# A streaming encoder step on one core: the norm ahead of a gated feed-forward layer, taken apart into a weight on its operand and a factor on its products

## The chip, the cores and the metric

The kernel runs on one core of a Trainium2 chip. The metric is the time of one execution on the device in microseconds (us), as the median of several runs. The engines are TensorE (PE; its weight loads are shown as PEld), VectorE (DVE), ScalarE (ACT), GpSimd (POOL) and SyncE (SP), which here only issues DMAs. Each engine works through its own instructions in order; semaphores order the engines among each other.

## What is computed

One layer over 1024 new frames and 32 frames of a running stream, 1056 tokens of 1024 features. The part that the change touches is the end of the layer:

```python
h = x + mixed @ w_out
z = rmsnorm(h, norm_ffn_g)
h = h + (jax.nn.silu(z @ w_gate) * (z @ w_up)) @ w_down

def rmsnorm(x, g):
    y = x * rsqrt(mean(x * x, axis=-1) + 1e-6)
    return y * g
```

`w_gate` and `w_up` are 1024 x 2816, `w_out` 1024 x 1024, `w_down` 2816 x 1024, all in float32. The norm multiplies each feature by its weight g and each token by one factor r = rsqrt(mean(h²) + 1e-6). The factor is the same for all features of a token.

## The kernel before

Activations lie feature by feature: 128 features on the partitions, tokens along the columns. A float32 product is made of three fp32r products: each operand is split into a high part (ScalarE's copy to fp32r) and a low part (the difference), and high·high, high·low and low·high are added in PSUM. `split`, `block` and `low_part` do that (lines 245, 248, 1417, 1418, 1676, 1684).

**Tokens in pairs.** From `attn_out` on, the 1056 tokens are cut into four chunks of `CW` = 264 columns, two for each half p = 0, 1. The buffers come from pools: `pa` (14) and `pb` (16) hold tiles of 4 x 264 columns (`Q`), `tp` holds eight of 2 x 264 (`D`), which pass the residual's columns xt, the squares sq, the factor's na and nr, and t, s, y of the products. PSUM has seven banks for products.

**Output projection** (`out_proj`, from line 1546). Sixteen tiles n, the eight output blocks j for p = 0, then for p = 1. For each of the two chunks c: 24 matmuls (line 1430), VectorE adds the residual xt to the bank and writes h (line 1602), SP stores h to memory (line 1604; the down projection reads it again), ScalarE squares it (line 1605). With c = 0 VectorE also makes the low part of the next tile's weights (line 1418) and adds up the squares (line 1563). The tile of xt for n + 1 is loaded at the start of tile n (line 1557). In tiles 1 to 7 the weights of the first two units of gate and up are prepared.

**The operand of gate and up** (`pair_operand`, lines 1633 to 1679) is a generator that is advanced a step at a time between other work. It multiplies ones by the squares on TensorE (line 1638), takes Ln and Exp on ScalarE for r (lines 1639 to 1642, with a Newton step on VectorE, lines 1643 to 1645), scales the sixteen blocks of h with g and r on VectorE (line 1659), and then forms seven operands z from sums and differences of the four quarters of h (`B_SUMS`, line 1667), each with its zh (ScalarE, line 1676) and zl (VectorE, line 1684). For p = 0 it runs from tile 8 of the output projection on, in the order `EARLY`; for p = 1 it runs between the products of unit 0 and of the first half of unit 1, in the order of `ORDER`. An ACT table set with Ln and Exp is loaded at the start of `out_proj` (line 1568).

**Gate and up** (`ffn_up`). A unit f is 128 columns of gate and the same of up. The 2 x 2 block product of weights [gate, up] and operand is made by seven products instead of eight (`seven_products`, line 1736: seven of 12 matmuls, 84 in all, into four banks a to d). Order: unit 0 with p = 0, units 1 to 21 each with p = 0 and p = 1, unit 0 with p = 1. After products 1, 5 and 2 ScalarE copies the bank to t (line 1740), since products 7, 3 and 4 go on in the same banks; POOL combines the copies (lines 1743, 1744); VectorE adds the banks (line 1726); ScalarE takes Silu (lines 1750, 1755) and VectorE multiplies it by up (lines 1752, 1756). SP stores y (line 1810). While one unit runs, the weights of the next are prepared: sums on VectorE (ws, line 1705), high parts on ScalarE, low parts on POOL.

```python
            if i == 3:
                nc.scalar.activation(y1, banks["b"], AF.Silu)
                add(t1, banks["b"], t1)
                nc.vector.tensor_mul(y1, t1, y1)
            if i == 4:
                add(t2, banks["c"], t2)
                nc.scalar.activation(y0, t2, AF.Silu)
                nc.vector.tensor_mul(y0, banks["c"], y0)
```

In this whole part, up to the end of `ffn_up`, the order on each of the five engines is the order of the program.

**Down projection** (`ffn_down`) loads the stored y (line 1846), splits it, and adds the products to h, in new pools that take over the buffers and banks of the old ones as these come free.

Of the kernel before, what the change touches and what calls it, by code (L numbers as in the profile page):

```python
# [10 lines left out]
AF = mybir.ActivationFunctionType  # L11
ALU = mybir.AluOpType
# [17 lines left out]
CW = 264  # L30
# [24 lines left out]
ORDER = (1, 5, 2, 6, 7, 3, 4)  # L55
EARLY = (1, 5, 7, 4, 3, 2, 6)

STEPS = {0: "s0", 1: "p0", 2: "s3", 3: "p3", 4: "s4", 5: "p4", 8: "s1", 9: "s2 p1", 10: "p2", 11: "p5", 13: "p6"}
STEPS_1 = {7: "s0", 8: "s3 p0", 9: "s4 p3", 10: "s1 p4", 11: "s2 p1", 12: "p2 p5", 13: "p6"}
FIRST = {1: "s0", 2: "s1 p0", 3: "s2 p1", 4: "s3 p2", 5: "s4 p3", 6: "p4", 7: "p5 p6"}  # L60
BANK = {1: "a", 5: "b", 2: "c", 6: "d", 7: "a", 3: "b", 4: "c"}
# [79 lines left out]
class Builder:  # L141
# [1404 lines left out]
    def out_proj(self, w):  # L1546


        nc = self.nc
        xts, accs = [], []  # L1550
        work = None
        self.z = [{}, {}]

        def xt_load(p, j):
            xts.append(self.D("xt"))
            o = 2 * CW * p
            nc.sync.dma_start(xts[-1].rearrange("p c n -> p (c n)"), self.xT[j, :, o:o + 2 * CW])

        def sum_squares():

            if len(accs) == 2:
                x = accs.pop()
                nc.vector.tensor_add(accs[0], accs[0], x)

        order = [(p, j) for p in range(2) for j in range(8)]
        xt_load(0, 0)

        nc.scalar.preload_act_table_set("natural_log_exp_and_others")
        def tile(dt, s):
            return self.Q(self.pa, dt, s).rearrange("p c n -> p (c n)")[:, 0:NP].rearrange("p (k n) -> p k n", n=P)  # L1570

        preps = []
        for f in range(2):
            r = [tile(F32, "raw") for _ in range(2)]
            for x, src in zip(r, self.units[f]):
                nc.sync.dma_start(x, src)
            preps.append(self.unit_weights(r, nc.vector, tile if f else [self.wx] * 7))
            r = x = None

        def store(steps):  # L1580

            out = preps[1](steps)
            for i in list(out):
                hi, lo = out.pop(i)
                for a, x in enumerate((hi, lo)):
                    nc.sync.dma_start(self.w1d[ORDER.index(i), :, 4 * a:4 * a + 4, :], f32(x))

        h = {}
        for n, (p, j) in enumerate(order):
            self.fetch(3)  # L1590
            if n + 1 < len(order):
                xt_load(*order[n + 1])
            wj, xt = w, xts.pop(0)
            w, low = self.block(True) if n + 1 < len(order) else (None, None)
            sq = self.D("sq")
            for c in range(2):
                if j % 4 == 0:
                    h[j // 4, c] = self.Q((self.pa, self.pb)[p], s="h")
                ps = self.psd()
                self.block_products(ps, wj, lambda k: (x[:, 2 * (k % 2) + c, :] for x in self.mx[p, k // 2]), CW)  # L1600
                x = h[j // 4, c][:, j % 4, :]
                nc.vector.tensor_add(x, ps[:, :CW], xt[:, c, :])
                o = CW * (2 * p + c)
                nc.sync.dma_start(self.hd[j, :, o:o + CW], x)
                nc.scalar.activation(sq[:, c, :], x, AF.Square)
                if c == 0:
                    if low:
                        low(nc.vector)
                    sum_squares()
                    if n in FIRST:  # L1610
                        preps[0](FIRST[n])
                    if n == 8:
                        work = self.pair_operand(0, h0, accs.pop(), EARLY)
                        h0 = None
                elif n in FIRST:
                    store(FIRST[n])
                for _ in range((c if n == 8 else 1 + c) if work else 0):
                    next(work, None)
            accs.append(sq)
            if j == 7:  # L1620
                for k in range(4):
                    del self.mx[p, k]
                if p == 0:
                    h0, h = h, {}
            if n == 14:
                self.turn = 0
                self.third = self.unit_load(2)
        sum_squares()
        for _ in work:
            pass  # L1630
        self.unit, self.work = preps[0](""), self.pair_operand(1, h, accs.pop(), ORDER)

    def pair_operand(self, p, h, acc, order):

        nc = self.nc
        a, r = self.D("na"), self.D("nr")
        for c, t in enumerate((self.pst(), self.psd())):
            nc.tensor.matmul(t[:, :CW], self.ones, acc[:, c, :], start=True, stop=True)
            nc.scalar.activation(r[:, c, :], t[:, :CW], AF.Ln, bias=self.eps_rms, scale=1.0 / 1024)
            nc.scalar.activation(a[:, c, :], t[:, :CW], AF.Identity, bias=self.eps_rms, scale=1.0 / 1024)  # L1640
        acc = None
        nc.scalar.activation(r, r, AF.Exp, scale=-0.5)
        nc.vector.scalar_tensor_tensor(a, a, -0.5, r, op0=ALU.mult, op1=ALU.mult)
        nc.vector.tensor_mul(a, a, r)
        nc.vector.scalar_tensor_tensor(r, a, 1.5, r, op0=ALU.add, op1=ALU.mult)
        a = None
        yield
        left = {q: sum(q in B_SUMS[i] for i in order) for q in h}
        normed = set()
        low = None  # L1650
        pool = (self.pa, self.pb)[p]
        for i in order:
            terms = B_SUMS[i]
            for q in terms[:2]:
                if q not in normed:
                    normed.add(q)
                    for k in range(4):
                        x = h[q][:, k, :]
                        nc.vector.scalar_tensor_tensor(x, x, self.g("norm_ffn_g", 4 * q[0] + k), r[:, q[1], :], op0=ALU.mult,  # L1659
                                                       op1=ALU.mult)  # L1660
                    yield
            if len(normed) == 4:
                r = None
            x = h[terms[0]]
            if len(terms) > 1:
                x = self.Q(self.pb, s="sum")
                nc.vector.tensor_tensor(x, h[terms[0]], h[terms[1]], terms[2])
            for q in terms[:2]:
                left[q] -= 1
                if left[q] == 0:  # L1670
                    del h[q]
            yield
            if low:
                self.low_part(p, pool, *low)
            hi = self.Q(pool, FR, "zh")
            nc.scalar.copy(hi, x)
            low = i, x, hi
            x = None
            yield
        self.low_part(p, pool, *low)  # L1680

    def low_part(self, p, pool, i, x, hi):
        lo = self.Q(pool, FR, "zl")
# [33 lines left out]
    def seven_products(self, w, p, between):  # L1717
# [4 lines left out]
        t, s, y = self.D("t"), self.D("t"), self.D("y")  # L1722
        t1, t2, t5 = t[:, 0, :], t[:, 1, :], s[:, 0, :]
        y0, y1 = y[:, 0, :], y[:, 1, :]
        copies = {1: t1, 5: t5, 2: t2}
        add = lambda out, a, b, op=ALU.add: nc.vector.tensor_tensor(out, a, b, op)  # L1726
        for i in ORDER:
# [19 lines left out]
            if i == 7:  # L1747
                add(t2, banks["a"], t2, ALU.subtract)
            if i == 3:
                nc.scalar.activation(y1, banks["b"], AF.Silu)  # L1750
                add(t1, banks["b"], t1)
                nc.vector.tensor_mul(y1, t1, y1)
            if i == 4:
                add(t2, banks["c"], t2)
                nc.scalar.activation(y0, t2, AF.Silu)
                nc.vector.tensor_mul(y0, banks["c"], y0)
        return y

    def unit_load(self, f):
# [17 lines left out]
    def ffn_up(self):  # L1777
# [7 lines left out]
        for n, f in enumerate(order):  # L1785
# [7 lines left out]
            for p in (0, 1) if 0 < n < NFF else (n > 0,):  # L1793

                def between():
                    nonlocal w, step
                    if prep and step in steps:
                        w = prep(steps[step])
                    step += 1
                    if n < 2 and p == 0 and n + step > 2:  # L1800
                        for _ in range(1 + (n + step > 3)):
                            next(work, None)

                if n == p == 1:
                    for _ in work:
                        pass
                y = self.seven_products(cur, p, between)
                o = 2 * CW * p
                queue = nc.scalar if n == NFF else nc.sync
                queue.dma_start(self.hidd[f, :, o:o + 2 * CW], y.rearrange("p c n -> p (c n)"))  # L1810
                y = None
            if n + 3 < len(order):
                raws.append(self.unit_load(order[n + 3]))
            cur = prep = None
        self.z = w = None

    def ffn_down(self, region):
        nc = self.nc
# [304 lines left out]
```

## Time and profile before

| | |
|---|---|
| median of 3 runs | 1569.53 us (1568.97 to 1569.88) |
| the profiled execution's own time | 1572.19 us |
| its span, first to last instruction | 1570.4 us |
| PE busy | 1513.8 us (96%) |
| DVE busy | 957.5 us (61%) |
| ACT busy | 593.2 us (38%) |
| POOL busy | 482.1 us (31%) |
| mean granted clock of TensorE | 0.985 of full speed |
| longest groups of the chain that ended last | matmuls of gate and up (line 1736) 26%, of output and down projection (line 1430) 18%, of the input projection (line 429) 11% |

A profile shows one execution; its time lies close to the median, and differences are formed against the execution itself. An engine's busy time says how much it has to do, not whether the end waits for it: for that, one looks for stretches in which TensorE, the busiest engine, stood idle, and for what released it.

### The profile page before, as it was taken

Reading aid. Unit: us, or ns where it says so; the run is one execution under the profiler, and the core shown is the slowest. Engines: PE = TensorE matmul, PEld = TensorE weight load, DVE = VectorE, ACT = ScalarE, POOL = GpSimd, SP = SyncE. Lnnn points to the kernel's source line nnn. Section 1 sums busy time; section 2 is a strip of 40 time slices with the busy share of each in tenths; the row PEclk is TensorE's granted clock in tenths of the full one; section 3 lists DMA queues with packets and bytes.
Section 4 is the critical chain, followed back from the end, with each engine's and each line's share of the span. In section 5 each row is a group of like instructions: output and inputs, shape, how many; then the busy total and the mean of one; then the engine's idle time right before and its main releaser. Section 6 shows DMA issues by size and latency. Waiting matters only on the chain.

```text
span 1570.4 us, 27321 instructions
## 1 busy us (share of the span) xinstructions
PE 1513.8 (96%) x10622; PEld 1477.1 (94%) x10622; DVE 957.5 (61%) x1743; ACT 593.2 (38%) x1219; POOL 482.1 (31%) x482
## 2 busy tenths in 40 slices
PE   8999999989999999988998999999999999999997
PEld 7999998979999998888997999999999999999996
DVE  7799998668776566355797544444444444234236
ACT  4411212375655444233543333333333342122115
POOL 2200000433432212310000655565555553122222
PEclk9999999999999999989999999999999999999999
DMA  8312232434633467856854222222222237223213
GB/s 251 120 41 81 87 100 75 132 76 134 203 105 112 119 208 223 266 185 184 262 151 159 82 80 70 71 75 82 82 82 82 82 102 232 83 79 112 84 63 111
DMA packets 212880, 193.54 MB, mean 123 GB/s; under 512 B 13018, under 2 KB 185846, under 8 KB 212751
## 3 DMA queue, kind: packets, MB, share of 16 engines
q1 hardware_dynamic: 212015, 189.91, 39.6%
q8 instruction: 83, 1.36, 0.4%
q0 software_dynamic: 576, 1.62, 0.3%
q14 instruction: 46, 0.38, 0.1%
q10 hardware_dynamic: 160, 0.27, 0.0%
HBM read 135.08 MB, written 56.68 MB: 122 GB/s over the span
## 4 chain that ended last, share of the span: by engine, by line
PE 65%; DVE 6%; ACT 3%; issue 3%; DMA 2%; POOL 1%; SPq 0%; DVEq 0%; ACTq 0%; POOLq 0%
PE pd L1736 26%; PE pd L1430 18%; PE pd L429 11%; PE po L1112 2%; PE ps L1073 2%; PE pt L1095 2%; PE pd L1899 1%; PE pt L251 1%; DVE gate L1495 1%; DMA xt<-xT 1%; DVE h L1659 1%; DVE ml L1499 1%; PE pd L1924 1%; DVE wlo L1418 1%; PE pt L1274 0%
## 5 line engine op out<-in xcount | busy, mean ns | idle before, releaser
L1736 PE MATMUL pd<-zh,whl 128*128 128x264 f32 x2464 | 455.6, 286 | 10.5 <-ACT t L1740 9.6
L1736 PEld LDWEIGHTS pd<-zh,whl 128*128 128x128 f32 x2464 | 386.3, 190 | 11.5 <-ACT t L1740 10.1
L1736 PE MATMUL pd<-zl,whl 128*128 128x264 f32 x1232 | 352.4, 286 | 0.0
L429 PE MATMUL pd<-xl,whi 128*128 128x352 f32 x832 | 270.6, 325 | 0.5 <-POOL xl L539 0.5
L429 PE MATMUL pd<-xh,whi 128*128 128x352 f32 x832 | 271.0, 326 | 0.0
L429 PE MATMUL pd<-xh,wlo 128*128 128x352 f32 x832 | 270.9, 326 | 0.0
L1736 PEld LDWEIGHTS pd<-zl,whl 128*128 128x128 f32 x1232 | 234.3, 190 | 0.0
L1726 DVE TENSOR_TENSOR t<-pd,t 128x264 f32<-128x264 f32 x176 | 75.4, 429 | 202.1 <-POOL t L1744 154.1
L248 POOL TENSOR_TENSOR whl<-ws,whl 128x512 fp32r<-128x512 f32 x105 | 135.6, 1292 | 147.9 <-ACT whl L245 147.9
L429 PEld LDWEIGHTS pd<-xl,whi 128*128 128x128 f32 x832 | 156.8, 188 | 2.0 <-POOL xl L539 0.8
L429 PEld LDWEIGHTS pd<-xh,whi 128*128 128x128 f32 x832 | 156.8, 188 | 1.4
L429 PEld LDWEIGHTS pd<-xh,wlo 128*128 128x128 f32 x832 | 156.8, 188 | 0.7
L766 DVE SCALAR_TENSOR_TENSOR acc<-cu,wdw,acc 128x1024 f32<-128x1024 f32 x120 | 147.3, 1284 | 0.2
L1875 DVE TENSOR_TENSOR h<-pd,h 128x352 f32<-128x352 f32 x96 | 49.7, 523 | 138.3 <-PE pd L1430 138.2
L1430 PE MATMUL pd<-hl,whi 128*128 128x352 f32 x360 | 116.1, 323 | 0.0
L1430 PE MATMUL pd<-hh,whi 128*128 128x352 f32 x360 | 116.1, 322 | 0.0
L1430 PE MATMUL pd<-hh,wlo 128*128 128x352 f32 x360 | 116.1, 322 | 0.0
L245 ACT CAST whl<-ws 128x512 fp32r<-128x512 f32 x115 | 71.4, 621 | 74.7 <-DVE ws L1705 72.1
L248 POOL TENSOR_TENSOR wlo<-raw,whi 128x1024 fp32r<-128x1024 f32 (+1 forms) x31 | 63.9, 2062 | 100.3 <-ACT whi L245 84.7
L245 ACT CAST whi<-raw 128x1024 fp32r<-128x1024 f32 (+1 forms) x47 | 45.0, 957 | 112.0 <-PE pd L429 79.2
L1418 POOL TENSOR_TENSOR wlo<-raw,whi 128x640 fp32r<-128x640 f32 x24 | 39.4, 1643 | 131.9 <-ACT whi L1417 117.0
L1743 POOL TENSOR_TENSOR t<-t,t 128x264 f32<-128x264 f32 x44 | 34.0, 773 | 146.3 <-ACT t L1740 146.3
(349 smaller groups left out, 3061.1 us busy)
## 6 DMA issues: line engine op xcount, KB each, us to landing
raw<-in_w_in SPq DMA_DIRECT2D x35, 512.0 KB, 4.0
hidd<-y SPq DMA_DIRECT2D x43, 264.0 KB, 2.0
hid<-hidd SPq DMA_DIRECT2D x18, 528.0 KB, 4.5
gd<-gate SPq DMA_DIRECT2D x48, 176.0 KB, 1.8
q<-qd SPq DMA_DIRECT2D x32, 256.0 KB, 5.0
raw<-in_w_down SPq DMA_DIRECT2D x24, 320.0 KB, 3.3
raw<-in_w_gate SPq DMA_DIRECT2D x13, 512.0 KB, 4.9
raw<-in_w_up SPq DMA_DIRECT2D x13, 512.0 KB, 4.7
```

Of the source, the lines that this page charges most:

```text
L245: nc.scalar.copy(hi, src)
L248: (lo_engine or nc.gpsimd).tensor_tensor(lo, src, f32(hi), ALU.subtract)
L429: nc.tensor.matmul(ps[:, :n], lhs, b, start=(m == 0), stop=(m == total - 1))
L766: nc.vector.scalar_tensor_tensor(acc[:, 0:NP], cu[:, j:j + NP], w(j), acc[:, 0:NP], op0=ALU.mult, op1=ALU.add)
L1073: nc.tensor.matmul(s[:, 512 * j:512 * j + e - o], q[:, m, qs], k[:, o:e], start=(m == 0), stop=(m == 1))
L1095: nc.tensor.transpose(t[:, o:o + P], lt[n, b][:, P * kb:P * kb + P], self.ident)
L1418: low = lambda engine: engine.tensor_tensor(lo, r, f32(hi), ALU.subtract)
L1430: self.nc.tensor.matmul(ps[:, :n], a[:, k, :], b, start=(m == 0), stop=(m == total - 1))
L1726: add = lambda out, a, b, op=ALU.add: nc.vector.tensor_tensor(out, a, b, op)
L1736: nc.tensor.matmul(banks[b], x[:, k, :], z[:, k, :], start=first and k == m == 0, stop=i not in copies and k == 3 and m == 2, skip_group_c ...
L1743: nc.gpsimd.tensor_tensor(t2, t2, t5, ALU.add)
L1875: nc.vector.tensor_add(s, ps[:, :CH], s)
```

## The change

The weight g and the factor r of the norm are taken apart. VectorE writes h into the buffer of xt, SP stores it from there, and ScalarE writes h·g as a copy with a scale for each partition. The operands z are formed from h·g without r, so `pair_operand` no longer waits for the factor and no longer scales. The factor r is made by a function of its own, `norm_factor`: for p = 0 in tile 8 as before, for p = 1 after the third product of unit 1 (before: of unit 0), and both stay in their `tp` buffers to the end of `ffn_up`. In `seven_products` gate is multiplied by r ahead of Silu, and the finished y by r once more, which is up's factor. Operand 2 of p = 1, the first of the new order `LATER`, is formed in tile 14 of the output projection. The steps of the generators are spread anew: one a chunk in the output projection, one a product in unit 0 and the first half of unit 1.

```diff
+LATER = (2, 1, 5, 6, 7, 3, 4)
...
-                x = h[j // 4, c][:, j % 4, :]
-                nc.vector.tensor_add(x, ps[:, :CW], xt[:, c, :])
+                x = xt[:, c, :]
+                nc.vector.tensor_add(x, ps[:, :CW], x)
                 o = CW * (2 * p + c)
                 nc.sync.dma_start(self.hd[j, :, o:o + CW], x)
+                nc.scalar.activation(h[j // 4, c][:, j % 4, :], x, AF.Copy, scale=self.g("norm_ffn_g", j))
                 nc.scalar.activation(sq[:, c, :], x, AF.Square)
...
                     if n == 8:
-                        work = self.pair_operand(0, h0, accs.pop(), EARLY)
+                        self.norm_factor(0, accs.pop())
+                        work = self.pair_operand(0, h0, EARLY)
                         h0 = None
...
-                for _ in range((c if n == 8 else 1 + c) if work else 0):
+                if work:
                     next(work, None)
+                    if n == 15:
+                        next(work, None)
+                if n == 13 and c:
+                    ahead = self.pair_operand(1, h, LATER, 1)
+                if n == 14:
+                    next(ahead)
...
-        self.unit, self.work = preps[0](""), self.pair_operand(1, h, accs.pop(), ORDER)
+        self.unit, self.work, self.squares = preps[0](""), ahead, accs.pop()
...
-                    for k in range(4):
-                        x = h[q][:, k, :]
-                        nc.vector.scalar_tensor_tensor(x, x, self.g("norm_ffn_g", 4 * q[0] + k), r[:, q[1], :], op0=ALU.mult,
-                                                       op1=ALU.mult)
-                    yield
...
             if i == 3:
-                nc.scalar.activation(y1, banks["b"], AF.Silu)
+                nc.vector.tensor_mul(y1, banks["b"], r[:, 1, :])
+                nc.scalar.activation(y1, y1, AF.Silu)
                 add(t1, banks["b"], t1)
                 nc.vector.tensor_mul(y1, t1, y1)
             if i == 4:
                 add(t2, banks["c"], t2)
-                nc.scalar.activation(y0, t2, AF.Silu)
+                nc.vector.tensor_mul(y0, t2, r[:, 0, :])
+                nc.scalar.activation(y0, y0, AF.Silu)
                 nc.vector.tensor_mul(y0, banks["c"], y0)
+                nc.vector.tensor_mul(y, y, r)
...
-                    if n < 2 and p == 0 and n + step > 2:
-                        for _ in range(1 + (n + step > 3)):
-                            next(work, None)
+                    if n < 2 and p == 0:
+                        next(work, None)
+                    if n == 1 and step == 3:
+                        self.norm_factor(1, self.squares)
+                        self.squares = None
```

## Rows read from the trace of the kernel before

**Rows 1.** Stretches: length, busy (x instructions) by engine, clock, DMA share, GB/s.

```profile
725.90:825.90 100.00, 97.51 (x771) 96.06 (x772) 78.49 (x123) 45.89 (x75) 0.00 (x0) 0.98 0.62 191
825.90:877.30 51.40, 40.87 (x285) 39.89 (x283) 38.42 (x55) 19.68 (x35) 12.31 (x12) 0.87 0.36 118
877.30:1293.00 415.70, 415.70 (x3418) 415.52 (x3418) 190.85 (x350) 157.65 (x353) 249.11 (x226) 1.00 0.28 81
```

**Rows 2.** Stretches of one product each, unit 1 and unit 2.

```profile
837.00:855.30 18.30, 13.21 (x85) 13.00 (x85) 15.49 (x27) 7.01 (x10) 1.58 (x2) 0.81 0.39 125
855.30:872.90 17.60, 13.05 (x88) 12.84 (x87) 14.71 (x18) 7.14 (x12) 5.50 (x5) 0.81 0.04 16
872.90:884.90 12.00, 11.11 (x88) 10.61 (x87) 6.79 (x10) 4.33 (x10) 9.36 (x9) 1.00 0.41 110
884.90:895.10 10.20, 10.20 (x86) 10.20 (x85) 6.00 (x12) 4.73 (x11) 5.96 (x7) 1.00 0.08 29
```

**Rows 3.** TensorE's waits, 825 to 880: total us, times, longest us.

```profile
PE pd L1736 <- ACT t L1740: 9.6, 2, 5.1
```

**Rows 4.** Stretches after two stops of TensorE.

```profile
848.00:854.00 6.00, 5.93 (x27) 5.93 (x28) 5.96 (x10) 1.65 (x4) 1.34 (x2) 0.50 0.80 220
1298.00:1301.50 3.50, 3.50 (x14) 3.50 (x13) 0.34 (x2) 0.62 (x1) 1.27 (x1) 0.52 0.91 251
```

**Rows 5.** Timeline of ScalarE: start us, duration us, instruction, idle before.

```profile
830.96 0.48 ACT L1639 ACTIVATE nr<-pt,eps_rms 128x264 f32<-128x264 f32 x1 [1.57 <-PE pt L1638]
832.43 0.66 ACT L1642 ACTIVATE nr<-nr 128x528 f32<-128x528 f32 x1
843.16 1.28 ACT L1750 ACT_TABLE_LOAD   x1
844.45 0.39 ACT L1750 ACTIVATE y<-pd 128x264 f32<-128x264 f32 x1
847.32 0.42 ACT L1755 ACTIVATE y<-t 128x264 f32<-128x264 f32 x1 [1.52 <-DVE t L1726]
847.65 0.64 ACT L1740 COPY t<-pd 128x264 f32<-128x264 f32 x2
```

**Rows 6.** Timeline of VectorE, units 0 and 1.

```profile
833.12 0.71 DVE L1643 SCALAR_TENSOR_TENSOR na<-na,nr 128x528 f32<-128x528 f32 x1 [4.96 <-ACT nr L1642]
836.22 3.32 DVE L1659 SCALAR_TENSOR_TENSOR h<-h,vec,nr 128x264 f32<-128x264 f32 x8
839.46 0.43 DVE L1726 TENSOR_TENSOR t<-pd,t 128x264 f32<-128x264 f32 x1
839.80 1.25 DVE L1667 TENSOR_TENSOR sum<-h,h 128x1056 f32<-128x1056 f32 x1
840.97 0.43 DVE L1726 TENSOR_TENSOR t<-pd,t 128x264 f32<-128x264 f32 x1
846.86 0.43 DVE L1726 TENSOR_TENSOR t<-pd,t 128x264 f32<-128x264 f32 x1
```

**Rows 7.** Timeline of ScalarE, the convolution's norm.

```profile
348.01 1.28 ACT L815 ACT_TABLE_LOAD   x1
350.32 1.28 ACT L820 ACT_TABLE_LOAD   x1
```

**Rows 8.** Timeline of VectorE, first weight sum for unit 2.

```profile
865.91 1.28 DVE L1705 TENSOR_TENSOR ws<-raw,raw 128x512 f32<-128x512 f32 x2
```

**Rows 9.** Timeline of ScalarE, a product of a later unit.

```profile
1008.79 0.38 ACT L1740 COPY t<-pd 128x264 f32<-128x264 f32 x1 [0.32 <-PE pd L1736]
```

**Rows 10.** Timeline into the down projection, SP's store and TensorE's wait.

```profile
1286.26 0.32 SPq L1810 DMA_DIRECT2D hidd<-y  x1
...
1297.69 0.43 PE L1430 MATMUL pd<-hh,whl 128*128 128x352 f32 x1 [1.93 <-DVE y L1756]
```

**Rows 11.** DMA issues, 735 to 826: count, KB each, median us to landing.

```profile
hd<-h SPq DMA_DIRECT2D x30, 132.0 KB, 3.0
xt<-xT SPq DMA_DIRECT2D x14, 264.0 KB, 4.4
```

More of the change, by code (lines that the diff above doesn't have):

```diff
@@ L1551, in out_proj @@
         work = None
-        self.z = [{}, {}]
+        self.z, self.r = [{}, {}], {}
         def xt_load(p, j):
@@ L1588, in out_proj @@
         h = {}
+        ahead = None
         for n, (p, j) in enumerate(order):
@@ L1630, in out_proj, with norm_factor @@
             pass
-        self.unit, self.work = preps[0](""), self.pair_operand(1, h, accs.pop(), ORDER)
-    def pair_operand(self, p, h, acc, order):
+        self.unit, self.work, self.squares = preps[0](""), ahead, accs.pop()
+    def norm_factor(self, p, acc):
         nc = self.nc
@@ L1640, in pair_operand @@
             nc.scalar.activation(a[:, c, :], t[:, :CW], AF.Identity, bias=self.eps_rms, scale=1.0 / 1024)
-        acc = None
         nc.scalar.activation(r, r, AF.Exp, scale=-0.5)
@@ L1645, in pair_operand @@
         nc.vector.scalar_tensor_tensor(r, a, 1.5, r, op0=ALU.add, op1=ALU.mult)
-        a = None
-        yield
-        left = {q: sum(q in B_SUMS[i] for i in order) for q in h}
-        normed = set()
+        self.r[p] = r
+    def pair_operand(self, p, h, order, early=0):
+        nc = self.nc
+        left = {q: sum(q in B_SUMS[i] for i in order) for q in ((0, 0), (0, 1), (1, 0), (1, 1))}
         low = None
         pool = (self.pa, self.pb)[p]
-        for i in order:
+        for n, i in enumerate(order):
             terms = B_SUMS[i]
-            for q in terms[:2]:
-                if q not in normed:
-                    normed.add(q)
-                    for k in range(4):
-                        x = h[q][:, k, :]
-                        nc.vector.scalar_tensor_tensor(x, x, self.g("norm_ffn_g", 4 * q[0] + k), r[:, q[1], :], op0=ALU.mult,
-                                                       op1=ALU.mult)
-                    yield
-            if len(normed) == 4:
-                r = None
             x = h[terms[0]]
@@ L1671, in pair_operand @@
                     del h[q]
-            yield
+            if len(terms) > 1:
+                yield
             if low:
@@ L1677, in pair_operand @@
             low = i, x, hi
-            x = None
+            x = hi = None
             yield
-        self.low_part(p, pool, *low)
+            if n < early:
+                self.low_part(p, pool, *low)
+                low = None
+                yield
+        if low:
+            self.low_part(p, pool, *low)
     def low_part(self, p, pool, i, x, hi):
@@ L1724, in seven_products @@
         y0, y1 = y[:, 0, :], y[:, 1, :]
+        r = self.r[p]
         copies = {1: t1, 5: t5, 2: t2}
@@ L1814, in ffn_up @@
             cur = prep = None
-        self.z = w = None
+        self.z = self.r = w = None
     def ffn_down(self, region):
```

## The prediction, made before the changed kernel was run

> **What bounds the kernel now.** I read the page first, then the chain of waits, then stretches and the timeline by engine. TensorE is the longest busy row by far, so time is won only where it stands idle or runs at half clock. By stage [rows 1], it is idle for 2.5 of the output projection's 100 us (725.9 to 825.9), most of it in that stage's start, which the change leaves alone; in units 2 to 21 of gate and up (877.3 to 1293) it is never idle; but in 825.9 to 877.3 it is busy for 40.9 of 51.4 us at a granted clock of 0.87. That stretch is where the second half's factor and operand are made. A product of 84 matmuls takes 10.20 us when nothing is late (the last of [rows 2]). Against that the first half of unit 1 lasted 18.3 (8.1 lost), its second half 17.6 (7.4 lost), the first half of unit 2 12.0 (1.8 lost): 17.3 us in all. In the first two, 9.6 us are two waits of TensorE, 5.1 and 4.5, for ScalarE's copy of a bank (t, L1740) [rows 3]. The other 5.9 are mostly the half clock behind each: 27 matmuls took 0.22 us apiece instead of 0.1215, at a granted 0.50, the 1.2 GHz level [rows 4].
>
> Why was the copy late? ScalarE works in order, and ahead of the copy (847.65) stood the second Silu (847.32), idle until VectorE's t (L1726) [rows 5]. VectorE had stood empty 4.96 us for the factor's Exp, then worked through three factor instructions, eight of sixteen scalings (L1659), a sum and two low parts before it came to that t at 846.86 [rows 6]. So VectorE, through ScalarE's queue, is what ends last there.
>
> **The change, part by part.** Starts below are chained from [rows 2, 5, 6], start to start where instructions overlap: on VectorE 1.17 for 1056 columns (839.80 to 840.97), 0.35 for 264, 0.405 for a scaling, 3.1 for the factor's three; on ScalarE 0.98 for 1056, 0.36 for Ln and its like, 0.53 for Exp, 1.28 for a table load; on TensorE 1.46 for twelve matmuls.
>
> *Unit 0.* VectorE loses its empty 4.96 us, the factor and the scalings; three sums, three low parts, four adds, the first y and two new multiplications by the factor remain, 9.9 us from 828.4, with 2.3 of waits for POOL and ScalarE. The second Silu then starts at 840.6 instead of 847.3, the copy at 840.9. TensorE, past the sums of squares (0.94, moved here), wants it at 842.9. The 5.1 us are gone, with 2.0 to spare.
>
> *Unit 1, first half.* VectorE still has the last y, the new y·r (0.62) and the sum for operand 3: ends 843.3. ScalarE's copy zh of it ends 844.3, and the copy for operand 5 behind it 844.7, wanted at 844.3: 0.4 lost. Now the second half's factor stands in ScalarE's queue, ahead of the copy for operand 2. Before, its Ln and Exp ran under a table set loaded in the output projection; now a Silu has run in between. In the convolution's norm, Ln (L815) after another function took a load, and Exp (L820) after that Ln a second [rows 7]. So: load 1.28, four instructions of 0.36, load 1.28, Exp 0.53, and the copy ends at 849.5, wanted at 846.2: 3.4 lost. The third load, for Silu, hides: VectorE is later.
> By the Trainium skill ("ScalarE: Activation LUTs", Table sets) one set holds both exp and ln, so Ln then Exp would need one load, and the sum below would be 1.3 us better. [Rows 7] show two in this kernel, which I take.
>
> *Unit 1, second half.* From 849.3 VectorE does the factor (3.1), two low parts (2.3) and ten short instructions with their waits; the second Silu starts at 857.8, the copy behind it at 858.1. TensorE, if its clock stays up, wants it at 856.8 (1.7 lost by its end, then 0.9 for the next copy); if the 3.4 us take the clock down, TensorE itself is later and loses about 2.6 in slow matmuls instead. After the 1.93 us before the down projection the clock was 0.52 [rows 4, 10]; I take it so. Either way 2.6.
>
> *Unit 2.* Its weights are prepared behind that: the first sum (ws) starts at 859.2, 4.6 us before unit 2 begins at 863.8; before it was 865.91 against 872.9, 7.0 ahead [rows 2, 8]. The 1.8 us lost there grow to about 4.
>
> Sum: 0.4 + 3.4 + 2.6 + 4 = 10.4 lost, against 17.3: **6.9 us won**. Ends: 14.3 (only 3 lost: Ln and Exp share a load, the clock holds, the weights are in time) and 1 (each late step half as long again).
>
> *Output projection.* VectorE loses 16 scalings (6.5 us) in its second half and gains one low part; ScalarE gains 32 copies. No row has that form; the nearest with a column as operand is Ln, 0.48 [rows 5], the nearest without is the copy of a bank, 0.32 start to start; I take 0.48, 15 us over 100 in which ScalarE is busy 46 [rows 1]. Behind a copy stand the square and the next block's high part, wanted some 3 us later by the low part: covered. If not, 0.4 us a tile, 6 us. VectorE's relief shortens TensorE's waits for a low part there by 0.3, my estimate from the 2.5 us of idle time. The residual's buffer now waits for its store; that is a rival below.
>
> *Units 2 to 21.* Three VectorE instructions a product, about 0.43 + 0.43 + 0.70, some 62 us over 416 in which VectorE is busy 191 and TensorE always [rows 1]. The tightest use is again the copy behind the second Silu: it stood idle 0.32 us for TensorE [rows 9], so a Silu 0.5 later moves it by 0.2, and TensorE wants it four blocks, 5.8 us, after its own part is done. Cost 0; if that cover of over 4 us were gone, 0.5 us on each of 39 products, 20 us. The factors keep two of eight buffers; a product uses three, so two products still fit. SP's store of y comes 1.1 us later and the raw loads behind it too; they are read a unit (20 us) later: 0.
>
> *Into the down projection.* Here nothing hides it. TensorE stood 1.93 us for the bank that VectorE's last y frees [rows 10], then ran at half clock. That bank is now free only after y0·r: 0.45 later. The ten loads of the hidden rows stand on SP behind the store of unit 21's y (1286.26) [rows 10], which waits for the new y·r: 0.7 later, and ScalarE's splits of them stand ahead of the last Silus. I take **1.2 lost**; ends 0.4 (the splits have slack) and 2.5 (both, and a changed order).
>
> Net: -6.9 - 0.3 + 1.2 = -6.0. The profiled execution took 1572.19, 0.17% over the median of 1569.53; the difference carries over: 1566.2 beside the profile, **1563.5** for the median.
>
> **The rivals.** *Only moved (0.18).* The factor's chain in unit 1 is longer than I chain it, since ScalarE now stands between two waits of TensorE: both loads cost as much again (2.6), or VectorE's fourteen short instructions stretch as the last two of the factor's three did (1.2 each where one alone takes 0.71, [rows 6]). Of the 6.9 between 1 and 3.9 are left: 1566.5 to 1569.5. Against: Silu started 1.29 us after its load did [rows 5].
> The Trainium skill (same page, What ACT_TABLE_LOAD costs) counts 2.66 us a switch with its drain, the rule for this rival; the row agrees with the load alone.
>
> *All gone (0.13).* Every late step fits: 1555 to 1558. For it: VectorE is then no longer what ScalarE waits for in unit 0. Against: the two loads.
>
> *Slower by the residual's buffer (0.08).* xt was free once VectorE had added; now it holds until the store has landed. If the next load got the buffer of the tile just left, SP would wait with all behind it: 0.9 for add and issue, 3.0 for the store, 4.4 for the load [rows 11], 8.3 us, of 9.9 until the low part behind the add is late (a tile and a half, 8.7, and 1.2 of slack). At medians that fits; from 1.6 us above them it decides, and at 2.2 above it costs 0.6 on each of 15 tiles, 9 us: 1573. Against: at most six of eight buffers live, so the oldest is two tiles back.
>
> **How the numbers follow.** The forecast, 0.61, spans 1559 to 1566.4. About 0.2% (3.1 us) is what a measurement here can tell from no change: faster is below 1566.4, slower above 1572.7. Faster 0.61 + 0.13 = 0.74, same 0.18, slower 0.08. The range leaves out the slower case and the tail of the best: 1557.5 to 1569.
>
> **What would show it.** In the profile after: no wait of TensorE for t near 843; a wait of 3 to 4 us two blocks on, behind two table loads; the next under 2 us; TensorE busy throughout 880 to 1285; VectorE's share up by some 3 points; a longer stop before the down projection. Wrong would be: TensorE waiting in units 3 to 21, SP waiting before xt, or one load around Ln and Exp.

## The result, and the profile after

The changed kernel takes **1583.52 us** (median of 6; 1581.19 to 1585.75) against 1569.25 for the kernel before beside it (6 runs): ratio 1.0090, 95% interval 1.0074 to 1.0105. It is 0.9% slower; the prediction was 1563.5 and at most 1569. The profiled execution took 1582.46 with a span of 1580.2 (before 1572.19 and 1570.4), so the two profiles differ by 9.8 us of span and the medians by 14.3: before was profiled in one of its slower executions, after in one of its faster, and the ledger below, which is of the spans, holds 4.5 us less than the medians do.

The page of the changed kernel, busy time by engine:

```profile
PE 1517.3 (96%) x10622; PEld 1477.4 (93%) x10622; DVE 1030.5 (65%) x1843; ACT 604.1 (38%) x1254; POOL 479.3 (30%) x482
```

TensorE does the same 10622 matmuls; no other engine is near full. TensorE's waits from the output projection into the down projection (waited for, total us, times, longest), after:

```profile
PE pd L1745 <- ACT t L1749: 12.6, 24, 4.0
PE pt L1648 <- DVE sq L1564: 3.0, 1, 3.0
PE pd L1431 <- DVE t L1735: 3.0, 1, 3.0
PE pd L1745 <- POOL whl L249: 1.9, 1, 1.9
```

The first answers to [rows 3], two waits that made 9.6; now they are 24, most of them of 0.2 us. The stretches that answer to [rows 1]: the output projection; the 51.4 us from the start of unit 0, which hold units 0 and 1 and part of unit 2; the rest of gate and up:

```profile
725.90:825.90 100.00, 95.18 (x746) 93.88 (x746) 72.29 (x104) 59.15 (x107) 0.00 (x0) 0.97 0.58 182
827.46:878.90 51.44, 44.61 (x329) 43.20 (x328) 36.50 (x50) 25.39 (x44) 17.37 (x15) 0.93 0.38 125
878.90:1302.35 423.45, 415.74 (x3374) 411.54 (x3374) 268.37 (x464) 148.15 (x346) 242.90 (x223) 1.00 0.27 78
```

TensorE is idle for 4.8 us of the output projection's stretch (2.5 before) and for 7.7 of the last one, where before it never was; in the second it does more in as long a stretch (329 matmuls, 285 before). TensorE's waits and first matmuls, in the timeline (start, duration, in brackets the idle time and what ended it):

```profile
781.12 1.25 PE L1648 MATMUL pt<-sq,ones 128*128 128x264 f32 x2 [2.97 <-DVE sq L1564]
846.60 0.39 PE L1745 MATMUL pd<-zh,whl 128*128 128x264 f32 x1 [0.58 <-ACT t L1749]
851.73 0.39 PE L1745 MATMUL pd<-zh,whl 128*128 128x264 f32 x1 [3.40 <-ACT t L1749]
1085.42 0.28 PE L1745 MATMUL pd<-zh,whl 128*128 128x264 f32 x1
1085.90 0.39 PE L1745 MATMUL pd<-zh,whl 128*128 128x264 f32 x1 [0.20 <-ACT t L1749]
1086.12 0.28 PE L1745 MATMUL pd<-zl,whl 128*128 128x264 f32 x1
1296.57 0.59 PE L1745 MATMUL pd<-zh,whl 128*128 128x264 f32 x1 [4.00 <-ACT t L1749]
1305.60 0.43 PE L1431 MATMUL pd<-hh,whl 128*128 128x352 f32 x1 [2.97 <-DVE t L1735]
```

These are, in order: tile 8 of the output projection; unit 1, twice; a unit in the steady state, with the matmul before the stop and the one behind it; the last product; the first matmul of the down projection. Each of units 3 to 21 has one such stop. It shows as 0.20 us of idle time but costs 0.46: from start to start the matmuls around it take 0.48 and 0.22 us, where the others take 0.12. Units 3 to 21 as a whole, from the first matmul of unit 3 to that of the last product, before:

```profile
894.76:1282.74 387.98, 387.98 (x3195) 387.98 (x3194) 175.82 (x325) 144.94 (x323) 231.70 (x212) 1.00 0.26 76
```

After:

```profile
890.72:1286.60 395.88, 392.17 (x3194) 388.18 (x3193) 252.47 (x437) 138.45 (x323) 228.12 (x210) 1.00 0.26 75
```

With stage bounds read from the first and last matmul of each stage in the two timelines, the 9.8 us come out so:

```
up to the output projection               -1.8   (not touched; differs from run to run)
output projection, 101.1 -> 104.5         +3.4   the wait in tile 8
units 0 to 2                              -5.6   (to the start of unit 3)
units 3 to 21, 20.42 -> 20.84 a unit      +7.9   19 units
last product                              +5.7   4.0 waited, the rest mostly at half clock
into the down projection, 0.7 -> 3.2      +2.5   the wait moved ahead of its first matmul
down projection to the end                -2.2   it no longer holds the 1.93 of [rows 10]
```

That is 9.9 of the 9.8, with the rounding of the bounds. What the change was forecast to win (units 0 to 2) it won for the most part; losses at three places, the output projection, the steady state and the stages' end, took it and 10 us more.

### The profile page after: what moved, and what is told of

Read it like the earlier page. It is cut to its first block, busy times and chain, and to the rows that moved or that the text cites. A ratio compares the mean times of both kernels' runs of the same rounds, so it can differ in the third digit from the quotient of the medians.

```text
span 1580.2 us, 27432 instructions
## 1 busy us (share of the span) xinstructions
PE 1517.3 (96%) x10622; PEld 1477.4 (93%) x10622; DVE 1030.5 (65%) x1843; ACT 604.1 (38%) x1254; POOL 479.3 (30%) x482
## 4 chain that ended last, share of the span: by engine, by line
PE 62%; DVE 7%; ACT 4%; issue 3%; DMA 2%; POOL 1%; SPq 0%; DVEq 0%; ACTq 0%; POOLq 0%
PE pd L1745 24%; PE pd L1431 18%; PE pd L430 11%; PE po L1113 2%; PE pt L1096 2%; PE ps L1074 2%; PE pd L1913 1%; DVE ws L1713 1%; ACT whl L246 1%; PE pt L252 1%; DMA hd<-xt 1%; DVE gate L1496 1%; POOL whl L249 1%; DVE ml L1500 1%; PE pd L1938 1%
## 5 line engine op out<-in xcount | busy, mean ns | idle before, releaser
L767 DVE SCALAR_TENSOR_TENSOR acc<-cu,wdw,acc 128x1024 f32<-128x1024 f32 x120 | 147.2, 1280 | 0.2
```

Source lines behind the costliest of these rows:

```text
L767: nc.vector.scalar_tensor_tensor(acc[:, 0:NP], cu[:, j:j + NP], w(j), acc[:, 0:NP], op0=ALU.mult, op1=ALU.add)
```

## The experiments

Two theories of the steady state's 0.42 us per unit stood against each other. **The loop**: the queues of VectorE, ScalarE and POOL work in order and wait for one another in a ring; the new multiplication at a product's end lengthened the ring past TensorE's own time. **Its rivals**: buffers (the factors hold two of eight, so a product waits for a tile), or VectorE's total work. Experiments were made as edits of the changed kernel.

**1. No factor on the up half.**

```diff
-                nc.vector.tensor_mul(y, y, r)
```

> The last multiplication of y by the factor is left out of the changed kernel (so up lacks its factor). Theory (a ring of queues): copy of a bank, POOL's sums, VectorE's adds, y, y times factor, the next weight sum, its high part on ScalarE and again a copy make a loop that takes 10.42 us a product where TensorE needs 10.20; without 0.65 us of it TensorE sets the pace: a unit takes 20.4 us, the waits for t in units 3 to 21 are gone, the wait of 4.0 us in the last product shrinks below 1.5, and the kernel takes 10 to 14 us less than the changed one. Rival (buffers): two of eight buffers kept by the factors set the pace: a unit stays at 20.84. Rival (ports): VectorE's instructions with two inputs from SBUF and POOL stretch each other: with one of two of these left, half is won, a unit takes 20.6.

Measured: 1570.14 us, ratio to before 1.0007 (0.9997 to 1.0016); 13.4 less than the changed kernel; a unit took 20.35 us (all paces are TensorE's: from the first matmul of a unit to that of the next, mean over units 3 to 21). The waits for t in units 3 to 21 and in the last product are gone; those in unit 1 and in tile 8 remain:

```profile
PE pd L1431 <- DVE t L1735: 4.1, 1, 4.1
PE pd L1745 <- ACT t L1749: 4.1, 2, 3.4
PE pt L1648 <- DVE sq L1564: 3.5, 1, 3.5
```

The factors still hold their buffers here, so buffers are not it.

**2. The same multiplication, later.** It is issued behind the third product of the next half, where VectorE's queue has time, and y's store with it.

```diff
-                nc.vector.tensor_mul(y, y, r)
...
+    def finish(self):
+        if self.tail:
+            y, r, queue, out = self.tail
+            self.tail = None
+            self.nc.vector.tensor_mul(y, y, r)
+            queue.dma_start(out, y.rearrange("p c n -> p (c n)"))
...
+                    if step % 7 == 3:
+                        self.finish()
...
-                queue.dma_start(self.hidd[f, :, o:o + 2 * CW], y.rearrange("p c n -> p (c n)"))
+                self.tail = y, self.r[p], nc.scalar if n == NFF else nc.sync, self.hidd[f, :, o:o + 2 * CW]
```

> The multiplication of y by the factor and y's store are issued behind the third product of the next half (where VectorE waits for POOL), not at the end of their own; at the end of unit 21 and in the last product at once. Theory (ring): the same instructions, but out of the loop: a unit takes 20.4 us as without the multiplication, the last product waits less than 2 us, 9 to 13 us less than the changed kernel. Rival (ports): the same two-input instructions run beside POOL, a unit stays at 20.8. Rival (buffers): y is held longer, a unit takes 20.84 or more.

Measured: 1569.49 us, ratio 1.0000 (0.9989 to 1.0012); a unit took 20.35. All instructions are there, VectorE is as busy as in the changed kernel (63 to 65 of each 100 us in both), and 14 us (9 to 13 expected) are won by the place alone. So buffers are not it here either, nor do VectorE's two-operand instructions and POOL's set the pace by stretching each other (the expectation's "ports"), by which a unit would have stayed at 20.8. Where the queues stand is seen in what ScalarE's copies of a bank wait for. Instruction groups of ScalarE from 910 to 1280: busy us and mean ns, then idle time before them and what ended it. The kernel before:

```profile
L1740 ACT COPY t<-pd 128x264 f32<-128x264 f32 x108 | 41.0, 380 | 70.0 <-PE pd L1736 70.0
```

The changed kernel:

```profile
L1749 ACT COPY t<-pd 128x264 f32<-128x264 f32 x105 | 35.5, 372 | 0.0
```

The factor deferred:

```profile
L1749 ACT COPY t<-pd 128x264 f32<-128x264 f32 x108 | 39.0, 372 | 9.9 <-PE pd L1745 9.6
```

Before, the copies stood idle for TensorE 70 us: the ring was ahead of it. In the changed kernel they never do: they find their bank ready every time, so ScalarE's queue is behind TensorE. Deferred, they wait for it again, though briefly, since the ring is late from units 0 to 2 and has to make that up: y0's last multiplication starts 14.9 us behind the first matmul of its product in unit 4 and is level, at 12.7, only from unit 11 on. In the changed kernel it stays 15.6 behind (first half of each unit in both).

**3. More of it, and less of it.** First the multiplication twice in a row, then the same work in two halves, the first where VectorE idles for ScalarE's Silu.

```diff
                 nc.vector.tensor_mul(y, y, r)
+                nc.vector.tensor_mul(y, y, r)
```

> Dose upwards. The multiplication of y by the factor at each product's end is issued twice in a row, so the up half carries its factor squared; nothing else differs from the changed kernel. Ring theory: the extra instruction lies on the loop of in-order queues that already runs slower than TensorE, so each product of units 2 to 21 gets longer by its issue time, 0.63 to 0.71 us; the pace of a unit goes from 20.84 to 22.1 to 22.25, 19 units add 24 to 27 us, and with the last products the time is 1608 to 1613 us. Rival, buffers or an overlap with other work (the instruction is hidden as the free 5 us of VectorE per product would allow): pace under 21.0, time 1583 to 1587. If VectorE's own total were the bound, the time would not change either, since its busy share is 65%.

```diff
+                nc.vector.tensor_mul(y1, y1, r[:, 1, :])
                 nc.vector.tensor_mul(y0, banks["c"], y0)
-                nc.vector.tensor_mul(y, y, r)
+                nc.vector.tensor_mul(y0, y0, r[:, 0, :])
```

> Dose downwards, same work. The factor's multiplication is cut in its two halves: y1 times r is issued between the gate multiplication of y0 and y0 itself, where VectorE idles 0.49 us in every product for ScalarE's Silu (0.49 <- ACT y at 1083.14 of the changed kernel), and only y0 times r, 0.34 us of issue for 0.63, stands behind the product's last multiplication. Ring theory: the loop gets shorter by about 0.3 us per product, from 10.42 to about 10.12, which is TensorE's own time; pace of a unit 20.2 to 20.4, the once-per-unit waits of 0.2 us for t gone, time 1571 to 1576. Rival, VectorE's number of instructions or its busy time decides: one more instruction per product and 0.13 us more busy time make it the same or slower, 1583 to 1590.

Measured: twice, 1613.93 us, ratio 1.0290 (1.0276 to 1.0304), a unit 22.31, just over what was expected. In halves, 1572.70, ratio 1.0027 (1.0017 to 1.0037), a unit 20.35. Stretches of 100 us in the middle of gate and up (busy us by engine in the order of [rows 1]), the changed kernel:

```profile
925.00:1025.00 100.00, 98.99 (x808) 97.94 (x807) 63.47 (x110) 35.39 (x83) 57.22 (x53) 1.00 0.25 73
```

Twice:

```profile
925.00:1025.00 100.00, 92.58 (x748) 90.98 (x747) 65.76 (x113) 32.84 (x77) 53.30 (x49) 1.00 0.27 78
```

In halves:

```profile
925.00:1025.00 100.00, 100.00 (x828) 100.00 (x827) 66.41 (x124) 35.92 (x84) 58.77 (x54) 1.00 0.28 81
```

Units 3 to 21 with the factor deferred (experiment 2):

```profile
887.68:1274.40 386.72, 386.72 (x3195) 386.72 (x3193) 246.83 (x441) 141.99 (x323) 242.27 (x212) 1.00 0.24 77
```

In halves:

```profile
891.19:1277.90 386.71, 386.71 (x3195) 386.71 (x3193) 258.47 (x479) 138.36 (x323) 229.34 (x211) 1.00 0.26 77
```

Without the factor they take 386.71 too: 20.35 a unit is what TensorE takes when nothing holds it. VectorE is busiest in the kernel whose TensorE is full, so its total work is not the bound. What counts is the time behind the product's last multiplication: when the factor's share of it goes from 0.63 us (start to start) to 1.37, a unit of two products grows by 1.48, which is 0.74 for each product. Back to 0.35, VectorE comes round in 20.29 us, 0.55 less and just under TensorE's 20.35: the start of y0's multiplication moves from 15.02 us behind the first matmul of its product in unit 4 to 13.95 in unit 21. It is still making up when the units end, so ScalarE's copies never wait for TensorE here either, though TensorE loses nothing (910 to 1280, in halves):

```profile
L1749 ACT COPY t<-pd 128x264 f32<-128x264 f32 x108 | 36.5, 372 | 0.0
```

**4. Where the ones matmuls stand in tile 8.** They are issued behind the tile's second chunk again, as before the change.

```diff
-                        self.norm_factor(0, accs.pop())
+                        squares = accs.pop()
...
+                if n == 8 and c:
+                    self.norm_factor(0, squares)
```

> One part undone: in tile 8 of the output projection the sums of squares are issued behind the second chunk's matmuls (as in the kernel before), not behind the first chunk's. Theory: TensorE's wait of 2.97 us there comes from that place alone, since the squares are summed on VectorE only behind tile 8's first chunk. Then the wait is gone, the output projection takes some 101.2 us again instead of 104.6, and the kernel takes 3 to 3.5 us less than the changed kernel; pace of a unit of gate and up stays 20.84. Rival: VectorE and ScalarE are the limit in tile 8 and the wait only moves to a low part of the weights: less than 1 us won.

Measured: 1579.31 us, ratio 1.0068 (1.0049 to 1.0088); the output projection took 100.0 us (104.5 in the changed kernel), 0.4 of the wait was left, and the steady state kept its pace (20.83). The 4.2 us (3 to 3.5 expected) come from this place: in the profiled executions the stage itself is 4.5 us shorter, while the 95% intervals of the two ratios overlap.

**5. Both undone.** Experiments 2 and 4 together.

> The ones matmuls of the first half behind the second chunk of tile 8 (as in the run with only this) and the factor deferred past the third product (as in that run), together. If the two losses are separate, the gains add: 1569.5 less the 3.2 to 4.2 of the ones alone gives 1565 to 1566.5, 0.2% under the kernel before. If they share one slack (the time won in tile 8 is given back in units 0 to 2), 1569 again.

Measured: 1567.23 us (11 runs), ratio 0.9987 (0.9978 to 0.9997). The two losses are separate, but 2.3 us were added, not the 3.2 to 4.2 expected: in the profiled execution of experiment 2 the output projection had taken 102.9 us, not 104.5, and here it takes 100.1, so 2.8 were to be had.

**6. The second half's factor in unit 0**, where Ln and Exp run under the set that is still loaded, first alone, then with both losses undone.

```diff
-                    if n == 1 and step == 3:
+                    if n == 0 and step == 3:
```

> One part undone: the second half's factor is formed behind the third product of unit 0 (as before the change), not of unit 1. Theory (table loads): the waits of 0.58 and 3.40 us in unit 1 come from the factor standing with two table loads ahead of the third copy; in unit 0 Ln and Exp run under the set already loaded, so both waits fall below 1 us together, ScalarE has two table loads less, and units 0 to 2 take 3 to 5 us less. Rival (backlog): VectorE waits empty for Exp in unit 0 again, as in the kernel before, and TensorE waits 2 to 5 us near the first products of unit 1: nothing won, or slower.

> As the run with both losses undone, and the second half's factor made behind the third product of unit 0, where Ln and Exp run with their table still loaded, in place of unit 1. From the run with this alone (2.1 us less up to unit 3): 1562.5 to 1565. If the wait of 3.4 us for ScalarE was not the table loads but the copies' place in the queue, it is the same as the run with both undone, 1565 to 1566.5.

Measured: alone 1580.55 us, ratio 1.0069 (1.0054 to 1.0084); with both undone **1564.90** (12 runs), ratio 0.9974 (0.9966 to 0.9983). The loads around Ln and Exp are gone, but TensorE's waits did not fall below 1 us together, as was expected: they are 2.08 and 1.77 us in place of 0.58 and 3.40, two shorter stops, and the clock stayed up behind them:

```profile
845.87 0.39 PE L1745 MATMUL pd<-zh,whl 128*128 128x264 f32 x1 [2.08 <-ACT t L1749]
849.36 0.39 PE L1745 MATMUL pd<-zh,whl 128*128 128x264 f32 x1 [1.77 <-ACT t L1749]
```

TensorE's stretch behind the second stop, the changed kernel:

```profile
852.00:858.00 6.00, 6.00 (x39) 6.00 (x39) 5.93 (x9) 2.03 (x3) 1.87 (x2) 0.72 0.00 0
```

The factor in unit 0 alone:

```profile
851.20:857.20 6.00, 6.00 (x52) 6.00 (x51) 4.63 (x9) 1.04 (x4) 1.41 (x1) 1.00 0.20 49
```

39 matmuls against 52 in 6 us, granted 0.72 against 1.00: what this experiment wins (2.1 us by unit 1's first y, where 3 to 5 were expected) is mostly the stretch at half clock (the 1.2 GHz level) after one stop of 3.4, not the waiting.

**7. One set by name.** With both losses undone and the factor in unit 1, ScalarE is told ahead of Ln which set to load.

```diff
+        if p:
+            nc.scalar.preload_act_table_set("natural_log_exp_and_others")
```

> As the run with both losses undone, and ahead of Ln in unit 1 the kernel asks by name for the one table set that is to hold Ln and Exp (one instruction on ScalarE; the loads that the compiler places follow from it). The changed kernel shows two loads of 1.28 us there, one before Ln and one before Exp, and TensorE waits 3.4 us behind them. If one set serves both, one load stands in the trace between Silu and Exp, the wait is 3.4 - 1.3 = 2.1 us, the clock behind it stays at 1.00 as behind the 2.1 us of the run with the factor in unit 0, and the time is 1.3 to 3 us under the run with both undone: 1564 to 1566. If Exp gets its own load in spite of it, two or three loads stand there, the wait is 3.4 to 4.7 us and the time 1567 to 1569.

Measured: 1564.41 us (10 runs), ratio 0.9971 (0.9958 to 0.9984). Timeline of ScalarE, the changed kernel (between the two loads only Ln and its like):

```profile
846.57 1.28 ACT L1649 ACT_TABLE_LOAD   x1
...
849.48 1.28 ACT L1651 ACT_TABLE_LOAD   x1
850.77 0.64 ACT L1651 ACTIVATE nr<-nr 128x528 f32<-128x528 f32 x1
```

With the set named:

```profile
841.70 1.28 ACT L1651 ACT_TABLE_LOAD   x1
843.00 0.48 ACT L1654 ACTIVATE nr<-pt,eps_rms 128x264 f32<-128x264 f32 x1
...
844.47 0.66 ACT L1656 ACTIVATE nr<-nr 128x528 f32<-128x528 f32 x1
```

One load serves both, and TensorE's wait there is 1.99 (3.40 with both losses undone and the set not named). The kernel before has the same instruction at the start of `out_proj` (line 1568), under which its Ln and Exp of [rows 5] ran without a load. That the clock would stay at 1.00 was wrong: it was 0.83 from 843 to 853.

## Why the prediction was wrong

**The step that failed is "Units 2 to 21: cost 0".** It followed one delay forward: the second Silu later, the copy behind it later by 0.2, TensorE four blocks away, "a cover of over 4 us". Each of these is right for one product. What it left out is that the delay comes round. Followed through one product of the changed kernel, VectorE first (start, duration, instruction, idle before):

```profile
1083.14 0.43 DVE L1767 TENSOR_TENSOR y<-pd,y 128x264 f32<-128x264 f32 x1 [0.49 <-ACT y L1766]
1083.60 0.71 DVE L1768 TENSOR_TENSOR y<-y,nr 128x528 f32<-128x528 f32 x1
1084.23 1.28 DVE L1713 TENSOR_TENSOR ws<-rawx,rawx 128x512 f32<-128x512 f32 x2
1088.51 0.43 DVE L1735 TENSOR_TENSOR t<-pd,t 128x264 f32<-128x264 f32 x1 [3.00 <-POOL t L1753]
...
1093.88 0.43 DVE L1767 TENSOR_TENSOR y<-pd,y 128x264 f32<-128x264 f32 x1 [0.49 <-ACT y L1766]
```

ScalarE in the same time:

```profile
1084.95 0.62 ACT L246 CAST whl<-ws 128x512 fp32r<-128x512 f32 x1 [1.57 <-DVE ws L1713]
1085.47 0.65 ACT L1749 COPY t<-pd 128x264 f32<-128x264 f32 x2
```

POOL in the same time:

```profile
1085.65 1.29 POOL L249 TENSOR_TENSOR whl<-ws,whl 128x512 fp32r<-128x512 f32 x1 [3.29 <-ACT whl L246]
1086.89 0.75 POOL L1752 TENSOR_TENSOR t<-t,t 128x264 f32<-128x264 f32 x1
1087.72 0.75 POOL L1753 TENSOR_TENSOR t<-t 128x264 f32<-128x264 f32 x1
```

y·r (1083.60) holds the weight sum behind it on VectorE (1084.23); the sum holds ScalarE's cast of it (1084.95), which stands ahead of two copies (1085.47); cast and copies hold POOL's low part and its two combinations of t (1085.65 to 1088.47); those hold VectorE's next add (1088.51, idle 3.00). From there VectorE is idle only twice, 0.21 and 0.49 us for Silu, until the next y0 and its y·r. Between this y0 multiplication and the next, 10.74 us pass and no engine waits for TensorE; the other product of the unit takes 10.10, together 20.84. TensorE alone needs 20.35 (experiments 1 and 2, and in halves). Slack toward TensorE was counted as if every product had it afresh; on a ring it is had once. Before, y0's multiplication started 11.6 us behind its product's first matmul; in the changed kernel it is 19.6 behind in unit 2, which itself takes 24.8 us, and from unit 3 on it stays at 15.6: the cover of 4 us is used up, and the pace is 20.84. The price given for a lost cover, 0.5 us on each of 39 products or 20 us, came out as 0.2 on each of 38 (7.9): most of the factor's 0.63 still fitted, the rest lay past the edge, and all of a second one does (0.74). That is borne out without the factor (experiment 1), where the ring makes up 1.0 and 0.8 us in units 3 and 4 and so, by an estimate from these, takes some 19.4 us a unit by itself.

**The last product and the way into the down projection: +1.2 predicted, +6.0 measured** (5.7 + 2.5 - 2.2). The mechanism named, hidden rows behind y's store, was one of two; the larger comes from the lag that the ring has built up. SP and ScalarE, changed kernel, each in its order:

```profile
1289.29 5.20 SPq L1394 DMA_DIRECT2D raw<-in_w_down  x2
1294.59 1.88 SPq L1860 DMA_DIRECT2D hid<-hidd  x4
1297.48 0.32 SPq L1824 DMA_DIRECT2D hidd<-y  x1
```

```profile
1292.12 0.62 ACT L1418 CAST whl<-raw 128x512 fp32r<-128x512 f32 x1 [6.97 <-DMA raw<-in_w_down]
1292.65 0.42 ACT L1760 ACTIVATE y<-y 128x264 f32<-128x264 f32 x1
1296.15 0.36 ACT L1749 COPY t<-pd 128x264 f32<-128x264 f32 x1
```

The load of the down weights starts at 1289.29 when POOL's last low part (done 1289.27) frees its buffer; before it was 1281.98. ScalarE's cast of it stands ahead of Silu (1292.65) and of the copies, and TensorE waits 4.00 for the first of them, then runs at a granted 0.53 (to 1300). The wait follows the ring's lag in unit 21: 4.88 us with the factor twice (17.1 behind), 4.00 in the changed kernel (15.6), 2.61 in halves (13.95), 1.41 deferred (12.7), none without the factor (12.3). But waits of 4.1 us (experiment 1) and 3.8 (experiment 2) before the down projection's first matmul remain; in experiment 2 VectorE's adds stand there behind low parts of the hidden rows. That wait was not taken apart.

**The output projection: -0.3 predicted, +3.4 measured.** The text took the first half's factor to be made in tile 8 as before, and the description of the change says the same. In the diff its call moved from a helper that the second chunk reaches to a line behind the first chunk. The ones matmuls in the kernel before stood without a wait:

```profile
782.74 0.61 PE L1638 MATMUL pt<-sq,ones 128*128 128x264 f32 x2
```

VectorE's sum of squares in the changed kernel:

```profile
780.37 0.70 DVE L1564 TENSOR_TENSOR sq<-sq,sq 128x528 f32<-128x528 f32 x1
```

After, TensorE reaches them one chunk earlier, before this sum is there, and stands 2.97 us, then runs slower. The priced item of that stage, the copy with a column scale, took 0.52 (0.48 taken) and was covered, as was said.

**Right:** the wait of 5.1 that the work of unit 0 had left behind is gone; in unit 1 the waits of 0.4 and 3.4 were 0.58 and 3.40, the longer one behind the two loads of 1.28 us; units 0 to 2 won 5.6 (6.9 predicted). The rule of the Trainium skill ("ScalarE: Activation LUTs", Table sets) that one set holds exp and ln holds here when the set is named (experiment 7), while two loads stand where it is left to each function; the prediction took the row, and the row was right for this kernel. The rival by the residual's buffer did not come about: no wait for it stood in the way of a matmul. Of the marks named beforehand, "TensorE waiting in units 3 to 21" is the one that came and cost; SP waited before xt once, 0.5 us, for ScalarE's square.

**What it could have been.** With the factor deferred, the ones matmuls moved back and one load or both of unit 1 avoided (experiments 6 and 7) the kernel takes 1564.90 and 1564.41, 0.26 and 0.29% under the kernel before: within 1.4 us of the forecast, but only with these three edits, and not by the forecast's account.

## What to carry to other kernels

When several in-order engines hand work round (VectorE to ScalarE to POOL to VectorE), follow a new instruction all the way round until it meets itself, and compare the sum with the bound engine's time for one turn: slack toward that engine is spent once, a surplus is paid at every turn. Whether the ring still has slack is read from what the small copies wait for: idle "<- PE" means room; none means that the ring is behind, and then the bound engine's own pace from unit to unit tells whether it is being held (20.84) or the ring is still making up a delay (20.35, in halves). An instruction that is needed late belongs behind the others' work or in a gap where its engine already waits (here at no cost to TensorE's pace), and a moved call is to be traced to where its matmuls now stand in TensorE's queue.

## What the runs showed that was not expected

- TensorE busy for 100% of a stretch was not TensorE at its pace: units 3 to 21 of the kernel before showed no idle time at 20.42 us each, but took 20.35 with the factor deferred. What held the kernel before by 0.07 us a unit (1.3 in all) was not tried.
- A pace is to be read on the engine that it is said of: with the factor deferred the starts of one VectorE instruction lie 20.23 us apart in the mean of units 4 to 20, because VectorE is making up a delay there, while TensorE takes 20.35 in every unit.
- A VectorE multiplication of two operands in SBUF took 0.43 us alone and about 1.07 beside POOL. From 895 to 1275 of the changed kernel L1765 ran 36 times: the 18 that began while POOL was at work took 1.06 us or more, the other 18 took 0.43 (1081.58 and 1092.96 are one of each). L1762 always began beside POOL there, as at 1091.51 beside the low part of 1091.01, and took 1.07 or more. That POOL is the cause was only read off, not tried.
- Two stops of TensorE of 2.1 and 1.8 us left the granted clock at 1.00, one of 3.4 took it to 0.72 over the next 6 us, and around one of 1.99 it was 0.83 over 10. Length of the stop alone does not tell which.
